# Two resident score buffers over five PSUM banks in the attention loop of a two-layer trunk

## The chip, the cores and the metric

The kernel runs on one core of a Trainium2 chip. The metric is device time in microseconds (us) from the first to the last instruction of one launch; lower is better. The core has a matrix engine (TensorE, PE in the rows; PEld is its weight load), a vector engine (VectorE, DVE), an activation engine (ScalarE, ACT), GpSimd (POOL) and a queue that issues DMAs (SyncE, SP). Matmul results land in PSUM, which has eight banks of 128 x 512 float32 each; VectorE and ScalarE read them there. TensorE's clock is granted at one of two levels, 1.2 or 2.4 GHz; the profile gives it as 0.5 or 1.0.

## The reference

Two layers over 1024 latent tokens and 256 context tokens of width 1024. Layer 0 is a gated linear recurrence beside a spatial gating unit. Layer 1 is a gated short convolution beside differential attention; the change lies in layer 1. Its attention, cut to what is needed here:

```python
def diff_attention(q, k, v, lam):          # 4 heads, two 64-wide maps m = 0, 1 per head
    s = jnp.einsum('bqhmd,bkhmd->bhmqk', q, k).astype(jnp.float32) * (DIFF_HEAD_DIM ** -0.5)
    p = jax.nn.softmax(s, axis=-1)          # over 1280 keys (256 context + 1024 latent)
    a = p[:, :, 0] - lam * p[:, :, 1]
    return jnp.einsum('bhqk,bkhe->bqhe', a.astype(v.dtype), v)
...
oo = rms_norm(oo, subln_g) * (1.0 - lam_init)
y_d = oo * jax.nn.silu(gate)                # then [y_c, y_d] @ w_out, residual, LayerNorm
```

Everything is float32. The kernel splits each float32 operand into a high and a low part (`split`: ScalarE makes the high part, VectorE or GpSimd subtracts for the low part) and multiplies with two or three matmuls.

## The kernel before

The program is one long list of instructions per engine. TensorE's order is the order of the code (`manual_schedule`); the other engines' orders are made by the scheduling layer, which also places the semaphore waits.

Layer 1 begins with projections for K and V (to about 602 us), then `run(proj_qg(0))`, the query and gate projection of head 0. Then comes the attention loop of 34 steps `i`, 32 of which work on one block of 128 queries of one head: `hd = i // 8`, block `i % 8`, `u = i % 2`. A step does, on TensorE:

- `scores(i, 0, st)`: six matmuls (128x256 or 128x512) that fill 1280 columns of a score tile `psc`. VectorE then takes the row maximum (`tensor_reduce`), and ScalarE the exponential of all 1280 columns with its row sum (`AF.Exp`, `accum_out`).
- for odd `i`, `av(i - 2)`: 30 matmuls of the probabilities with V into a bank `pav`; for even `i` sometimes `finish2` and `finish3`, the normalisation of a finished half head (`pms`, `prs`).
- `scores(i, 1, st)`: the second map. After it VectorE combines the two maps in `E0[i]`.
- `trans(i - 1, ..., j)` for j = 0, 1, 2: ten 128x128 transposes of the block before, four, four and two to a bank `atr`; each bank is read by ScalarE (`ah`) and VectorE (`al`).

Between these pieces `fill(us)` advances `fillers`, generators that project the other heads' queries and gates (`proj_qg`) and the convolution branch (`conv_branch`). A projection (`proj1_g`) is 24 matmuls of 128x512 into one bank, in eight groups of three. Fillers that are left when the loop ends run during the loads of the output weights (`out_weights`), before the output projection (`pout`).

Before the change the score tile `psc` is one buffer of three banks (`pa`), projections have two banks of their own (`pb`), and transposes, `pav`, `pms` and `prs` take turns in three banks: two of `ps1` (`psb`) and one of `pa` (`ps3`). K for one map is fetched into `kd` and split into `KS[m]` in one function, `load_k`; `kd` has one buffer, which `load_v` uses too.

Of the kernel before, what the change touches and what calls it, by code (L numbers as in the profile page):

```python
# [21 lines left out]
NTOK = CTX + LAT  # L22
KT = D // 128
# [19 lines left out]
def tile_hybrid_trunk(es: ExitStack, tc: tile.TileContext, A, out, scr=None):  # L43
# [110 lines left out]
    def run(gen):  # L154
        for _ in gen:
            pass
# [23 lines left out]
    def proj1_g(o, w, c0, n):  # L180
        hh, hl_ = hs(c0, n)
        for k in range(KT):
            hi, lo = w[k // 4]
            T.matmul(o, hi[:, k % 4], hh[:, k], start=k == 0, stop=False)  # L184
            T.matmul(o, hi[:, k % 4], hl_[:, k], start=False, stop=False)  # L185
            T.matmul(o, lo[:, k % 4], hh[:, k], start=False, stop=k == KT - 1)  # L186
            yield 0.65 * n / 512

    def proj1(o, w, c0, n):
# [559 lines left out]


    mask = [(i + 16) % 32 for i in range(32)]
    pa_cm, pb_cm = pool("pa", PSUM), pool("pb", PSUM)
    pbp, pa = pb_cm.__enter__(), pa_cm.__enter__()

    def pb(name):
        t = pbp.tile([128, 512], F32, name=name, tag="pb", bufs=2)
        return t

    kv_cm = pool("kv", side="right")
    kv = kv_cm.__enter__()  # L760
# [92 lines left out]
    def conv_branch(f):  # L853
# [25 lines left out]
        for c0 in (0, 512):  # L879
# [5 lines left out]
            V.tensor_tensor(u[:, c0:c0 + 512], u[:, c0:c0 + 512], s, op=ALU.mult)  # L885
            SY.dma_start(yc_d[f][:, c0:c0 + 512], u[:, c0:c0 + 512])

    ab_cm = pool("att")
    ap = ab_cm.__enter__()
    dl = ap.tile([128, 4, 64], F32, name="dl")  # L890
# [9 lines left out]
    gsub = lv[:, 6:7]  # L900
    V.tensor_scalar(gsub, P("subln"), 0.5 * (1.0 - LAM_INIT), None, op0=ALU.mult)

    def load_k(hd, m):
        kd = ap.tile([128, NTOK], F32, name="kd", tag="kd", bufs=1)
        for i in range(2):
            SY.dma_start(kd[64 * i:64 * i + 64], k_d[hd][64 * m:64 * m + 64])
        kt = ap.tile([128, NTOK], F32R, name=f"k{m}")
# [4 lines left out]
    def load_v(hd):  # L912
        vf = ap.tile([128, NT, 128], F32, name="vf", tag="kd", bufs=1)
        SY.dma_start(vf, v_d[:, :, 128 * hd:128 * hd + 128])
        vh = ap.tile([128, NT, 128], F32R, name="vh")
        vl = ap.tile([128, NT, 128], F32R, name="vl")
        split(vh, vl, vf, le=G)
        VS[0] = vh, vl

    def load_q(hd, pr):  # L920
# [17 lines left out]
            except StopIteration:  # L938
                fillers.pop(0)

    KS, VS, QS, AH, OF, SD = {}, {}, {}, {}, {}, {}

    turn = [0]

    def ps3(name):
        turn[0] += 1
        if turn[0] % 3:
            return psb(name)
        t = pa.tile([128, 512], F32, name=name, tag="ps3", bufs=1)
        return t  # L950

    def scores(i, m, st):
        hd, pr, u = i // 8, i % 8 // 2, i % 2
        qh, ql = QS[hd, pr]
        cu = slice(128 * u, 128 * u + 128)
        p = pa.tile([128, 1536], F32, name="psc", tag="psc", bufs=1)
        for c, n in CHUNKS:
            o = p[:, 256 + c:256 + c + n]
            T.matmul(o, qh[:, m, cu], KS[m][:, c:c + n], start=True, stop=False)  # L959
            T.matmul(o, ql[:, m, cu], KS[m][:, c:c + n], start=False, stop=True)  # L960
        V.tensor_reduce(st[:, m:m + 1], p[:, 256:1536], axis=AX.X, op=ALU.max, negate=True)  # L961
        e_ = ap.tile([128, NTOK], F32, name="e", tag="e", bufs=3)
        S.activation(e_, p[:, 256:1536], AF.Exp, bias=st[:, m:m + 1], scale=1.0, accum_out=st[:, 2 + m:3 + m])  # L963
# [60 lines left out]
    run(proj_qg(0))  # L1024
    fillers += [proj_qg(1), conv_branch(0), proj_qg(2), conv_branch(1), proj_qg(3), conv_branch(2), conv_branch(3)]
    load_k(0, 0)
    load_k(0, 1)
    E0, fin = {}, None
    for i in range(34):
        hd, pr, u = i // 8, i % 8 // 2, i % 2  # L1030
        if i < 32:
            if u == 0:
                QS[hd, pr] = load_q(hd, pr)
            st = ap.tile([128, 8], F32, name="st", tag="st", bufs=3)
            if i % 4 == 0:
                SD[i // 4] = ap.tile([128, 4], F32, name="sd", tag="sd", bufs=2)
            E0[i] = scores(i, 0, st)
            if i % 8 == 7 and hd < 3:
                load_k(hd + 1, 0)
        if i > 1 and u == 1:  # L1040
            fill(FL[1])
            av(i - 2)
            if i % 4 == 1:
                fin = ((i - 2) // 8, (i - 2) % 8 // 4, finish1((i - 2) // 8, (i - 2) % 8 // 4))
            if i % 8 == 1 and hd < 4:
                load_v(hd)
            fill(FL[2])
        elif fin is not None:
            fill(FL[0])
            fin2 = fin[0:2] + finish2(2 * fin[0] + fin[1], *fin[2])  # L1050
            fill(FL[3] - FL[0] - FL[8])
            finish3(*fin2)
            fill(FL[8])
            fin = None
        else:
            fill(FL[3])
        if i < 32:
            e1 = scores(i, 1, st)
            V.scalar_tensor_tensor(E0[i], e1, st[:, 6:7], E0[i], op0=ALU.mult, op1=ALU.add)
            if i % 8 == 7 and hd < 3:  # L1060
                load_k(hd + 1, 1)
        if i == 1:
            load_v(0)
# [27 lines left out]
    pb_cm.__exit__(None, None, None)  # L1091


    with pool("out1") as op, pool("po1", PSUM) as po:
# [148 lines left out]
```

## Time and profile before

| | |
|---|---|
| time, median of 3 runs (lowest to highest) | 1166.85 us (1166.33 to 1167.54) |
| the profiled execution: its time, its span | 1171.65 us, 1169.9 us |
| TensorE busy, share of the span | 1131.7 us, 97% |
| VectorE, ScalarE, GpSimd busy | 736.3, 440.3, 316.7 us |
| attention loop in the span | from 624 us to about 1046 us |
| mean granted clock of TensorE | 0.990 |

The rows of the trace give times in us from the start of the span of the profiled execution. Matmuls are pipelined: each row of one is longer than the distance to the next row's start, so for matmuls the distance between starts is the cost. A bracket such as [1.94 <-ACT e L963] says that the engine was idle for 1.94 us before that instruction, and what ended the wait.

### The profile page before, as it was taken

What the parts mean: (1) busy time and instruction counts of PE and PEld (TensorE: products, weight loads), DVE (VectorE), ACT (ScalarE), POOL (GpSimd) and SP (SyncE); (2) the same over time, 40 slices, a digit from 0 to 9 for tenths busy, and PEclk for the clock granted to TensorE, in tenths of its full rate; (3) what the DMA queues carried; (4) which work ended last, traced back from release to release, by engine and by line L of the source; (5) the groups of instructions that cost most, each with busy time, mean ns of one, the idle gap of its engine ahead of it and who ended that gap; (6) DMA issues with size and microseconds to landing.
All of it is one profiled execution on the core that took longest, in us unless ns stands there. A gap on an engine that the chain in (4) does not pass through costs nothing.

```text
span 1169.9 us, 14909 instructions
## 1 busy us (share of the span) xinstructions
PE 1131.7 (97%) x5842; PEld 925.4 (79%) x5842; DVE 736.3 (63%) x1007; ACT 440.3 (38%) x685; POOL 316.7 (27%) x200
## 2 busy tenths in 40 slices
PE   6999999999999999999998999999999899999997
PEld 3767777878888888888887888788788788888776
DVE  5677976943512665644015678786867777738897
ACT  3453654610221333341123555455534454413110
POOL 1111111630240222375014112222212121221971
PEclk9999999999999999999998999999989999999999
DMA  9654552230331534333126213222311410127622
GB/s 371 236 190 141 180 182 70 92 95 1 111 143 45 188 124 139 135 113 131 45 64 194 72 36 94 79 77 64 102 39 45 146 53 20 49 76 249 212 99 82
DMA packets 71095, 133.92 MB, mean 114 GB/s; under 512 B 5857, under 2 KB 34401, under 8 KB 70129
## 3 DMA queue, kind: packets, MB, share of 16 engines
q1 hardware_dynamic: 71024, 132.97, 33.9%
q8 instruction: 46, 0.75, 0.3%
q14 instruction: 25, 0.20, 0.0%
HBM read 105.67 MB, written 27.28 MB: 114 GB/s over the span
## 4 chain that ended last, share of the span: by engine, by line
PE 62%; DVE 7%; DMA 4%; POOL 3%; ACT 2%; issue 2%; SPq 0%; POOLq 0%; DVEq 0%; ACTq 0%
PE p L184 4%; PE p L185 4%; PE p L186 4%; PE pout L666 4%; PE pout L664 4%; PE pout L665 4%; PE pv L208 3%; PE pv L210 3%; PE pv L209 3%; PE psc L959 3%; PE psc L960 3%; PE atr L982 2%; POOL xres L1111 2%; PE pav L994 2%; PE pav L995 2%
## 5 line engine op out<-in xcount | busy, mean ns | idle before, releaser
L141 POOL TENSOR_TENSOR wlo<-wraw,whi 128x512 fp32r<-128x512 f32 x92 | 137.9, 1504 | 478.7 <-ACT whi L138 462.0
L666 PE MATMUL pout<-woh,ylo 128*128 128x512 f32 (+1 forms) x296 | 114.5, 387 | 3.8 <-DVE ylo L141 3.8
L961 DVE TENSOR_REDUCE st<-psc 128x1 f32<-128x1280 f32 x64 | 95.1, 1486 | 32.2 <-PE psc L960 32.1
L664 PE MATMUL pout<-woh,yhi 128*128 128x512 f32 (+1 forms) x296 | 114.8, 388 | 0.2
L665 PE MATMUL pout<-wol,yhi 128*128 128x512 f32 (+1 forms) x296 | 114.1, 385 | 0.0
L963 ACT ACTIVATE e<-psc,st 128x1280 f32<-128x1280 f32 x64 | 85.1, 1330 | 71.9 <-DVE st L961 71.2
L138 ACT ACTIVATE whi<-wraw 128x512 fp32r<-128x512 f32 x92 | 57.2, 627 | 135.9 <-PE p L185 31.6
L184 PE MATMUL p<-hhl,whi 128*128 128x512 f32 x256 | 105.7, 413 | 0.0
L186 PE MATMUL p<-hhl,wlo 128*128 128x512 f32 x256 | 101.5, 396 | 0.0
L185 PE MATMUL p<-hll,whi 128*128 128x512 f32 x256 | 101.2, 395 | 0.0
L959 PE MATMUL psc<-k,qh 128*128 128x512 f32 (+1 forms) x192 | 68.6, 372 | 12.7 <-ACT e L963 12.6
L960 PE MATMUL psc<-k,ql 128*128 128x512 f32 (+1 forms) x192 | 70.0, 365 | 0.0
L666 PEld LDWEIGHTS pout<-woh,ylo 128*128 128x128 f32 x296 | 55.6, 188 | 16.0 <-DVE ylo L141 4.6
L138 ACT ACTIVATE ah<-atr 128x512 fp32r<-128x512 f32 (+1 forms) x96 | 47.0, 525 | 52.2 <-PE atr L982 51.2
L664 PEld LDWEIGHTS pout<-woh,yhi 128*128 128x128 f32 x296 | 55.6, 188 | 12.3 <-issue 0.5
L665 PEld LDWEIGHTS pout<-wol,yhi 128*128 128x128 f32 x296 | 55.7, 188 | 11.4
L138 ACT ACTIVATE yhi<-yraw 128x512 fp32r<-128x512 f32 x36 | 22.5, 630 | 111.4 <-PE pout L665 62.2
L141 DVE TENSOR_TENSOR al<-atr,ah 128x512 fp32r<-128x512 f32 (+1 forms) x96 | 54.6, 593 | 6.1 <-ACT ah L138 5.9
L186 PEld LDWEIGHTS p<-hhl,wlo 128*128 128x128 f32 x256 | 48.7, 190 | 10.8
L185 PEld LDWEIGHTS p<-hll,whi 128*128 128x128 f32 x256 | 49.0, 191 | 8.6
L184 PEld LDWEIGHTS p<-hhl,whi 128*128 128x128 f32 x256 | 48.9, 191 | 8.4
L959 PEld LDWEIGHTS psc<-k,qh 128*128 128x128 f32 x192 | 36.6, 191 | 22.5 <-ACT e L963 17.9
(319 smaller groups left out, 2890.4 us busy)
## 6 DMA issues: line engine op xcount, KB each, us to landing
wraw<-in_w_in_dram SPq DMA_DIRECT2D x44, 512.0 KB, 4.5
wm<-in_w_mod_dram SPq DMA_DIRECT2D x64, 256.0 KB, 2.9
wraw<-in_w_out_dram SPq DMA_DIRECT2D x16, 512.0 KB, 3.6
wm<-in_w_mod_dram SPq DMA_DIRECT2D x7, 1024.0 KB
xt<-in_xcT_dram SPq DMA_DIRECT2D x8, 640.0 KB, 10.1
xres<-in_xc_dram SPq DMA_DIRECT2D x10, 512.0 KB, 3.7
kd<-k_d SPq DMA_DIRECT2D x16, 320.0 KB, 4.7
wvr<-in_w_v_dram SPq DMA_DIRECT2D x8, 512.0 KB, 3.6
```

What stands on the lines that cost most here:

```text
L138: S.activation(hi, src, AF.Copy)
L141: le.tensor_tensor(lo, src, f32(hi), op=ALU.subtract)
L184: T.matmul(o, hi[:, k % 4], hh[:, k], start=k == 0, stop=False)
L185: T.matmul(o, hi[:, k % 4], hl_[:, k], start=False, stop=False)
L186: T.matmul(o, lo[:, k % 4], hh[:, k], start=False, stop=k == KT - 1)
L664: T.matmul(o, hi[:, i], wh[:, c], start=first and i == 0, stop=False)
L665: T.matmul(o, hi[:, i], wl[:, c], start=False, stop=False)
L666: T.matmul(o, lo[:, i], wh[:, c], start=False, stop=not first and i == 3)
L959: T.matmul(o, qh[:, m, cu], KS[m][:, c:c + n], start=True, stop=False)
L960: T.matmul(o, ql[:, m, cu], KS[m][:, c:c + n], start=False, stop=True)
L961: V.tensor_reduce(st[:, m:m + 1], p[:, 256:1536], axis=AX.X, op=ALU.max, negate=True)
L963: S.activation(e_, p[:, 256:1536], AF.Exp, bias=st[:, m:m + 1], scale=1.0, accum_out=st[:, 2 + m:3 + m])
```

## The change

It has five parts.

1. `psc` becomes one resident tile `PSC` of 2560 columns, five banks: score 0 has columns 0 to 1279, score 1 columns 1280 to 2559. The third bank (columns 1024 to 1535) holds the last 256 columns of score 0 and the first 256 of score 1. The pieces of score 0 are written in the order 512, 512, 256, those of score 1 as before in the order 256, 512, 512.
2. The three other banks serve projections, transposes, `pav`, `pms` and `prs` together: `psb` gives out the one used longest ago, leaving out the bank of a projection that is under way. Before the loop (the K, V and first query projections) six banks rotate; then a pool is closed, and `PSC` is laid over its place.
3. The transposes move from behind score 1 to between the two scores, with fills of 1.4 and 0.4 around them; after score 1 only `fill(1.6 if u else 2.0)` is left.
4. K tiles are fetched two to three steps ahead (`fetch_k`, `kd` with two buffers), V right after a head's last step, and queries one step ahead. V's low part moves from GpSimd to VectorE, in two halves.
5. The square in `finish1` moves from VectorE to ScalarE.

```diff
@@ proj1_g, at the last k
+            if k == KT - 1:
+                bank["n"] += 1
+                last[bank["p"]] = bank["n"]
+                bank["p"] = None
@@
-    def psb(name="psb"):
-        t = ps1.tile([128, 512], F32, name=name, tag="psb", bufs=2)
+    def psb(name="psb", proj=False):
+        bank["n"] += 1
+        free = [b for b in last if b != bank["p"]]
+        b = min(free, key=last.get)
+        last[b] = bank["n"]
+        if proj:
+            bank["p"] = b
+        t = (ps1 if b < 2 else bank["pool"]).tile([128, 512], F32, name=name, tag=f"psb{b}", bufs=1)
         return t
@@
+    run(proj_qg(0))
+    pk_cm.__exit__(None, None, None)
+    for b in range(3, 6):
+        del last[b]
...
+    PSC = pa.tile([128, 2 * NTOK], F32, name="psc")
@@ load_v
-        split(vh, vl, vf, le=G)
+        for k in (0, 5):
+            split(vh[:, k:k + 5], vl[:, k:k + 5], vf[:, k:k + 5])
@@ scores
-        p = pa.tile([128, 1536], F32, name="psc", tag="psc", bufs=1)
-        for c, n in CHUNKS:
-            o = p[:, 256 + c:256 + c + n]
+        p = PSC[:, NTOK * m:NTOK * m + NTOK]
+        for c, n in (CHUNKS if m else ((0, 512), (512, 512), (1024, 256))):
+            o = p[:, c:c + n]
@@ finish1
-        V.tensor_tensor(sq, of, of, op=ALU.mult)
+        S.activation(sq, of, AF.Square)
@@ the loop
         if i > 1 and u == 1:
-            fill(FL[1])
+            fill(0.9)
             av(i - 2)
...
-            fill(FL[2])
+            fill(0.4)
...
         else:
-            fill(FL[3])
+            fill(3.6)
+        for js, us in (((0, 1), 1.4), ((2,), 0.4)):
+            for j in js:
+                if 1 <= i < 33:
+                    trans(i - 1, E0[i - 1], j)
+            fill(us)
         if i < 32:
             e1 = scores(i, 1, st)
...
-        fill(FL[4])
-        for js, us in (((0, 1), FL[5] + FL[6]), ((2,), FL[7])):
-            for j in js:
-                if 1 <= i < 33:
-                    trans(i - 1, E0[i - 1], j)
-            fill(us)
+        fill(1.6 if u else 2.0)
```

The first place is the end of a step on TensorE. Before, this is what stands behind score 1 of a step (`psc` from `k_4866`, the K tile of map 1): the rows begin at the last matmul of score 1 and end at the third piece of the transposes; three more projection matmuls follow, and then score 0 of the next step.

```order
L960 MATMUL psc<-k_4866,ql 128x512
L982 MATMUL atr<-ident,e 128x128 x8
L184 MATMUL p_5320<-hhl,whi 128x512
L185 MATMUL p_5320<-hll,whi 128x512
L186 MATMUL p_5320<-hhl,wlo 128x512
L184 MATMUL p_5320<-hhl,whi 128x512
L185 MATMUL p_5320<-hll,whi 128x512
L186 MATMUL p_5320<-hhl,wlo 128x512
L184 MATMUL p_5320<-hhl,whi 128x512
L185 MATMUL p_5320<-hll,whi 128x512
L186 MATMUL p_5320<-hhl,wlo 128x512
L982 MATMUL atr<-ident,e 128x128 x2
```

After the change the same place, with the semaphores that an instruction waits for; `k_4875` is the K tile of map 1, `k_4872` that of map 0.

```order
L984 MATMUL psc<-k_4875,ql 128x512
L184 MATMUL pg_5007<-hhl,whi 128x512
L185 MATMUL pg_5007<-hll,whi 128x512
L186 MATMUL pg_5007<-hhl,wlo 128x512 [waits Pool_49]
L184 MATMUL pg_5007<-hhl,whi 128x512
L185 MATMUL pg_5007<-hll,whi 128x512
L186 MATMUL pg_5007<-hhl,wlo 128x512
L184 MATMUL pg_5007<-hhl,whi 128x512
L185 MATMUL pg_5007<-hll,whi 128x512
L186 MATMUL pg_5007<-hhl,wlo 128x512
L983 MATMUL psc<-k_4872,qh 128x512 [waits Activation_49]
L984 MATMUL psc<-k_4872,ql 128x512
```

The transposes and a group of projection matmuls are gone from here, and the first matmul of score 0, which writes the first bank of `PSC`, waits for ScalarE. This wait stands in all 31 steps that follow another; the count it waits for is the one that the exponential of score 1 of the step before brings about. Nine projection matmuls stand between the two scores in 22 of these steps, six in eight and twelve in one. Over the whole loop, 897 projection matmuls stand between the first and the last score after the change, 861 before.

The second place is the transposes of an odd step after the change, behind the products with V (`pav`); `p_5158` is a projection.

```order
L1020 MATMUL pav<-ah,vl 128x256
L184 MATMUL p_5158<-hhl,whi 128x512
L185 MATMUL p_5158<-hll,whi 128x512
L186 MATMUL p_5158<-hhl,wlo 128x512
L1006 MATMUL atr<-ident,e 128x128 [waits DVE_49]
L1006 MATMUL atr<-ident,e 128x128 x3
L1006 MATMUL atr<-ident,e 128x128 [waits Activation_49]
L1006 MATMUL atr<-ident,e 128x128 x3
L184 MATMUL p_5158<-hhl,whi 128x512
L185 MATMUL p_5158<-hll,whi 128x512
L186 MATMUL p_5158<-hhl,wlo 128x512 [waits Pool_49]
```

Each bank of transposes now has a wait of its own for the engine that reads the bank's last content; before, the first eight transposes of a step stand behind a score, and in most steps without a wait.

The third place is SP's queue at the end of the loop: before, the last four loads of the output weights (`wraw` from `in_w_out_dram`) with what follows them; `xres` are the residual tiles, `yraw` the two branches' outputs, `rowln` the LayerNorm rows.

```order
L239 DMA wraw<-in_w_out_dram 128x1024 x2
L886 DMA yc_d<-uc 128x512
L1099 DMA rowln_g_8741<-in_ln_g_dram 128x1024
L239 DMA wraw<-in_w_out_dram 128x1024
L1099 DMA rowln_g_8743<-in_ln_g_dram 128x1024
L239 DMA wraw<-in_w_out_dram 128x1024
L1099 DMA rowln_b_8745<-in_ln_b_dram 128x1024
L1099 DMA rowln_b_8747<-in_ln_b_dram 128x1024
L886 DMA yc_d<-uc 128x512
L1110 DMA xres<-n_d 128x1024 x2
L250 DMA yraw<-yc_d 128x4x128
L1110 DMA xres<-n_d 128x1024
```

After the change, the same queue from the last LayerNorm row on.

```order
L1131 DMA rowln_b_8692<-in_ln_b_dram 128x1024
L1142 DMA xres<-n_d 128x1024 x2
L252 DMA wraw<-in_w_out_dram 128x1024
L1142 DMA xres<-n_d 128x1024
L899 DMA yc_d<-uc 128x512
L1142 DMA xres<-n_d 128x1024 x4
L899 DMA yc_d<-uc 128x512
L1142 DMA xres<-n_d 128x1024
L252 DMA wraw<-in_w_out_dram 128x1024
L263 DMA yraw<-yc_d 128x4x128 x2
L263 DMA yraw<-yd_d 128x4x128
L252 DMA wraw<-in_w_out_dram 128x1024
```

Three of the eight loads of the output weights now stand behind residual tiles, the last two behind all eight of them.

## Rows read from the trace of the kernel before

**Rows 1.** Page, part 1: busy us, share of the span, instructions of each engine.

```profile
PE 1131.7 (97%) x5842; PEld 925.4 (79%) x5842; DVE 736.3 (63%) x1007; ACT 440.3 (38%) x685; POOL 316.7 (27%) x200
```

**Rows 2.** Windows, attention loop and after: us, busy of each engine, clock, DMA share, GB/s.

```profile
624.00:1045.60 421.60, 408.31 (x2228) 346.83 (x2227) 297.92 (x413) 198.93 (x333) 88.65 (x58) 0.98 0.24 73
1045.60:1069.30 23.70, 23.70 (x108) 19.60 (x107) 22.21 (x24) 9.06 (x12) 2.58 (x2) 1.00 0.58 178
```

**Rows 3.** Waits of TensorE in the loop: us in total, times, longest.

```profile
PE psc L959 <- ACT e L963: 12.6, 9, 3.7
PE prs L1019 <- POOL rr L1011: 0.6, 1, 0.6
```

**Rows 4.** Groups by line, the two readers of a score: busy, mean ns | idle before.

```profile
L961 DVE TENSOR_REDUCE st<-psc 128x1 f32<-128x1280 f32 x64 | 95.1, 1486 | 32.2 <-PE psc L960 32.1
L963 ACT ACTIVATE e<-psc,st 128x1280 f32<-128x1280 f32 x64 | 85.1, 1330 | 71.9 <-DVE st L961 71.2
```

**Rows 5.** Timeline, one long wait for a score buffer: start us, us, engine, line.

```profile
741.38 0.39 PE L184 MATMUL p<-hhl,whi 128*128 128x512 f32 x1
...
741.61 0.40 PE L185 MATMUL p<-hll,whi 128*128 128x512 f32 x1
...
743.01 0.39 PE L960 MATMUL psc<-k,ql 128*128 128x512 f32 x1
743.04 3.27 DVE L1002 TENSOR_TENSOR sq<-of 128x512 f32<-128x512 f32 x1 [1.94 <-ACT of L997]
...
746.24 1.48 DVE L961 TENSOR_REDUCE st<-psc 128x1 f32<-128x1280 f32 x1
...
747.75 1.33 ACT L963 ACTIVATE e<-psc,st 128x1280 f32<-128x1280 f32 x1 [2.21 <-DVE st L961]
...
748.97 0.19 ACT L963 ACTIVATION_READ_ACCUMULATOR e<-psc,st 128x1 f32 x1
...
749.22 0.38 PE L959 MATMUL psc<-k,qh 128*128 128x256 f32 x1 [1.94 <-ACT e L963]
```

**Rows 6.** Timeline, a score whose readers are free, and two banks of transposes.

```profile
806.77 0.40 PE L960 MATMUL psc<-k,ql 128*128 128x512 f32 x1
...
807.01 1.04 PE L982 MATMUL atr<-ident,e 128*128 128x128 f32 x8
807.21 1.49 DVE L961 TENSOR_REDUCE st<-psc 128x1 f32<-128x1280 f32 x1 [0.39 <-PE psc L960]
...
807.64 1.09 ACT L138 ACTIVATE ah<-atr 128x512 fp32r<-128x512 f32 x2 [2.82 <-PE atr L982]
808.62 1.28 DVE L141 TENSOR_TENSOR al<-atr,ah 128x512 fp32r<-128x512 f32 x2
```

**Rows 7.** Windows, the stretches at half clock: the first of four, and their sum.

```profile
633.80:640.60 6.80, 6.02 (x15) 4.86 (x16) 4.66 (x12) 2.64 (x5) 3.87 (x3) 0.50 0.61 184
...
sum 20.40, PE 19.62 PEld 15.94 DVE 15.07 ACT 5.07 POOL 6.46; mean PE 4.90 PEld 3.99 DVE 3.77 ACT 1.27 POOL 1.61
```

**Rows 8.** Timeline, three of TensorE's nine waits for a score buffer.

```profile
634.58 0.58 PE L959 MATMUL psc<-k,qh 128*128 128x256 f32 x1 [3.71 <-ACT e L963]
...
712.76 0.39 PE L959 MATMUL psc<-k,qh 128*128 128x256 f32 x1 [1.08 <-ACT e L963]
...
847.94 0.39 PE L959 MATMUL psc<-k,qh 128*128 128x256 f32 x1 [1.97 <-ACT e L963]
```

**Rows 9.** Timeline, the readers of a gate projection's bank as the loop begins.

```profile
623.67 0.58 ACT L849 ACTIVATE sg<-pg 128x512 f32<-128x512 f32 x1
...
624.41 0.68 DVE L850 SCALAR_TENSOR_TENSOR sg<-sg,pg 128x512 f32<-128x512 f32 x1
```

**Rows 10.** Windows, the start of the output stage: columns as in rows 2.

```profile
1070.00:1090.00 20.00, 17.91 (x79) 14.44 (x78) 11.17 (x10) 4.61 (x6) 12.12 (x5) 1.00 0.98 347
```

**Rows 11.** Timeline, SP's queue in the output stage, and TensorE's first wait there.

```profile
1071.56 0.38 SPq L239 DMA_DIRECT2D wraw<-in_w_out_dram  x1
...
1073.76 1.16 SPq L1110 DMA_DIRECT2D xres<-n_d  x2
...
1089.08 0.50 PE L666 MATMUL pout<-woh,ylo 128*128 128x512 f32 x1 [2.09 <-DVE ylo L141]
```

More of the change, by code (lines that the diff above doesn't have):

```diff
@@ L212, in vtile @@
                 next(between, None)
-    def psb(name="psb"):
-        t = ps1.tile([128, 512], F32, name=name, tag="psb", bufs=2)
+    bank = {"n": 0, "p": None}
+    last = {0: 0, 1: 0}
+    def psb(name="psb", proj=False):
[6 more added lines that the diff above has]
+        t = (ps1 if b < 2 else bank["pool"]).tile([128, 512], F32, name=name, tag=f"psb{b}", bufs=1)
         return t
@@ L751, in tile_hybrid_trunk @@
     mask = [(i + 16) % 32 for i in range(32)]
-    pa_cm, pb_cm = pool("pa", PSUM), pool("pb", PSUM)
-    pbp, pa = pb_cm.__enter__(), pa_cm.__enter__()
+    pk_cm = pool("pk", PSUM)
+    bank["pool"] = pk_cm.__enter__()
+    last.update({b: 0 for b in range(2, 6)})
     def pb(name):
-        t = pbp.tile([128, 512], F32, name=name, tag="pb", bufs=2)
-        return t
+        return psb(name, True)
     kv_cm = pool("kv", side="right")
@@ L886, in conv_branch @@
             SY.dma_start(yc_d[f][:, c0:c0 + 512], u[:, c0:c0 + 512])
+    run(proj_qg(0))
+    pk_cm.__exit__(None, None, None)
+    for b in range(3, 6):
+        del last[b]
+    bank["p"] = None
+    pa_cm = pool("pa", PSUM)
+    pa = pa_cm.__enter__()
+    bank["pool"] = pa
+    PSC = pa.tile([128, 2 * NTOK], F32, name="psc")
     ab_cm = pool("att")
@@ L901, in tile_hybrid_trunk, with fetch_k, load_k @@
     V.tensor_scalar(gsub, P("subln"), 0.5 * (1.0 - LAM_INIT), None, op0=ALU.mult)
-    def load_k(hd, m):
-        kd = ap.tile([128, NTOK], F32, name="kd", tag="kd", bufs=1)
+    def fetch_k(hd, m):
+        kd = ap.tile([128, NTOK], F32, name="kd", tag="kd", bufs=2)
         for i in range(2):
             SY.dma_start(kd[64 * i:64 * i + 64], k_d[hd][64 * m:64 * m + 64])
+        KD[m] = kd
+    def load_k(m):
+        kd = KD.pop(m)
         kt = ap.tile([128, NTOK], F32R, name=f"k{m}")
@@ L910, in load_k, with fetch_v, load_v @@
         KS[m] = kt
-    def load_v(hd):
-        vf = ap.tile([128, NT, 128], F32, name="vf", tag="kd", bufs=1)
+    def fetch_v(hd):
+        vf = ap.tile([128, NT, 128], F32, name="vf", tag="kd", bufs=2)
         SY.dma_start(vf, v_d[:, :, 128 * hd:128 * hd + 128])
+        KD["v"] = vf
+    def load_v():
+        vf = KD.pop("v")
         vh = ap.tile([128, NT, 128], F32R, name="vh")
         vl = ap.tile([128, NT, 128], F32R, name="vl")
-        split(vh, vl, vf, le=G)
+        for k in (0, 5):
+            split(vh[:, k:k + 5], vl[:, k:k + 5], vf[:, k:k + 5])
         VS[0] = vh, vl
@@ L939, in fill @@
                 fillers.pop(0)
[L941 to L950, printed above, removed]
+    KS, VS, QS, AH, OF, SD, KD = {}, {}, {}, {}, {}, {}, {}
+    ps3 = psb
     def scores(i, m, st):
@@ L1022, in finish3 @@
         SY.dma_start(yd_d[hd][:, 512 * half:512 * half + 512], of)
-    run(proj_qg(0))
     fillers += [proj_qg(1), conv_branch(0), proj_qg(2), conv_branch(1), proj_qg(3), conv_branch(2), conv_branch(3)]
-    load_k(0, 0)
-    load_k(0, 1)
+    fetch_k(0, 0)
+    fetch_k(0, 1)
+    QS[0, 0] = load_q(0, 0)
+    load_k(0)
+    load_k(1)
+    fetch_v(0)
     E0, fin = {}, None
@@ L1031, in tile_hybrid_trunk @@
         if i < 32:
-            if u == 0:
-                QS[hd, pr] = load_q(hd, pr)
+            if u == 1 and i < 31:
+                QS[(i + 1) // 8, (i + 1) % 8 // 2] = load_q((i + 1) // 8, (i + 1) % 8 // 2)
+            if hd < 3 and i % 8 == 5:
+                fetch_k(hd + 1, 0)
+            if hd < 3 and i % 8 == 6:
+                fetch_k(hd + 1, 1)
             st = ap.tile([128, 8], F32, name="st", tag="st", bufs=3)
@@ L1038, in tile_hybrid_trunk @@
             if i % 8 == 7 and hd < 3:
-                load_k(hd + 1, 0)
+                load_k(0)
         if i > 1 and u == 1:
-            fill(FL[1])
+            fill(0.9)
             av(i - 2)
@@ L1045, in tile_hybrid_trunk @@
             if i % 8 == 1 and hd < 4:
-                load_v(hd)
-            fill(FL[2])
+                load_v()
+            fill(0.4)
         elif fin is not None:
-            fill(FL[0])
+            fill(0.7)
             fin2 = fin[0:2] + finish2(2 * fin[0] + fin[1], *fin[2])
-            fill(FL[3] - FL[0] - FL[8])
+            fill(2.9)
             finish3(*fin2)
-            fill(FL[8])
             fin = None
         else:
-            fill(FL[3])
+            fill(3.6)
[4 more added lines that the diff above has]
+            fill(us)
         if i < 32:
@@ L1060, in tile_hybrid_trunk @@
             if i % 8 == 7 and hd < 3:
-                load_k(hd + 1, 1)
+                load_k(1)
+                fetch_v(hd + 1)
         if i == 1:
-            load_v(0)
-        fill(FL[4])
-        for js, us in (((0, 1), FL[5] + FL[6]), ((2,), FL[7])):
-            for j in js:
-                if 1 <= i < 33:
-                    trans(i - 1, E0[i - 1], j)
-            fill(us)
+            load_v()
+        fill(1.6 if u else 2.0)
     fill(FL[0])
@@ L1090, in tile_hybrid_trunk @@
     pa_cm.__exit__(None, None, None)
-    pb_cm.__exit__(None, None, None)
+    del last[2]
+    bank["p"] = None
     with pool("out1") as op, pool("po1", PSUM) as po:
```

4 lines of the change are left out of this document (2 added, 2 removed).

## The prediction

> **What bounds the kernel now.** I read the page first: TensorE is busy for 97% of the span [rows 1], so time can come only from its idle time, from its clock, or go to new waits on it. The windows show where its idle time lies [rows 2]: in the attention loop it is busy for 408.31 of 421.60 us, idle for 13.3; the 23.7 us behind the loop, where the remaining projections run, have none. The waits name what it waits for [rows 3]: 12.6 us in nine waits for the exponential that reads the one score buffer, and 0.6 us once for GpSimd. The timeline shows how such a wait comes about [rows 5]: score 1 ends near 743.4, but VectorE is in the square of `finish1` (3.27 us) until 746.3, so the maximum runs at 746.24, the exponential at 747.75, and the next score 0 starts at 749.22, after 1.94 us of idleness. Last I looked at the clock: four stretches of the loop, 20.4 us together, have a granted clock of 0.5, the lower level [rows 7], and the first follows a wait of 3.71 us [rows 8]. The waits of 1.94, 1.97 and 2.45 us were followed by such a stretch too, that of 1.08 us wasn't.
>
> **What the change can give.** All waits of the loop are 12.6 + 0.6 = 13.2 us. The slow stretches hold 19.62 us of matmul work [rows 7], which at the full level would take half: 9.8 us. So the most that can be won in the loop is 23.0 us.
>
> **What it adds: a wait at each score 0.** Two buffers free score 0 from score 1 only if score 0 doesn't wait for the reader of score 1. As built it does: its first matmul waits for the exponential of the score 1 just before, in 31 steps. So what matters is how long that takes after score 1, and what TensorE does meanwhile. With free readers the chain is: the last matmul of score 1 starts at 806.77, the maximum at 807.21, 0.44 later [rows 6]; the maximum takes 1.49 [rows 4, 6]; the exponential follows 0.03 later (746.24 + 1.48 to 747.75), and from its start to the released matmul pass 749.22 - 747.75 = 1.47, which includes the read of the row sum [rows 5]. Sum: 0.44 + 1.49 + 0.03 + 1.47 = 3.43 us from the start of the last matmul. TensorE's own next slot is 0.23 after it (741.38 to 741.61) [rows 5], so 3.20 us must be covered.
>
> Before, ten transposes (eight take 0.8 us, from 807.01 to the next matmul) and 12 to 15 projection matmuls stood there: 1.0 + 12 x 0.23 = 3.8 us, enough unless a reader was late. Now nine, six or twelve projection matmuls stand there: 2.07, 1.38 or 2.76 us. The waits are 1.13 (22 steps), 1.82 (8) and 0.44 (once): 24.9 + 14.6 + 0.4 = 39.9 us. That is the floor, with both readers idle when a score ends. They aren't always: VectorE is busy for 297.92 of the loop's 421.6 us (0.71) and ScalarE for 198.93 (0.47) [rows 2]; with half of a typical 0.8 us instruction left on either, a score would wait 0.71 x 0.4 + 0.47 x 0.4 = 0.47 us more, 15 us over 31 steps. The square and the early fetches take load and late data out of this queue, V's low part puts some in; between 0 and 15 I take 8. **Term: +48 (40 to 55).**
>
> **Fewer banks.** Projections, transposes and `pav` now share three banks, one of which a projection holds. The second bank of transposes needs the bank that `pav` or an older piece has just left, the third piece that of the first. The trace has no such sharing; the nearest rows are the two banks at 807 [rows 6]: transposes start at 807.01, their first bank is free when half of VectorE's 1.28 us from 808.62 is done, 809.26, so 1.46 us after the eighth transpose's slot ends (807.80). The fill that now stands there is 1.4 us: 0.1 of wait if nothing is in the way. If ScalarE is inside an exponential (1.33 us [rows 4], up to once per step), up to 1.4 more. With ScalarE busy for 0.47 of the time and half an exponential left, 0.3; so 0.4 us for each of 32 blocks, 13 us, and 3 for projections that start in a bank just used. **Term: +16 (0 to 45).**
>
> **Start of the loop.** `PSC` lies over banks of the closed pool, so the first score waits until the last gate projection is read: 0.58 on ScalarE and 0.68 on VectorE [rows 9] with hops of the size above, 1.6 us on TensorE. **Term: +1.6 (0 to 4).**
>
> **Behind the loop.** 36 projection matmuls more (897 against 861) stand in the loop, 36 x 0.23 = 8.3 us. This moves work and costs nothing by itself, but the 23.7 us that cover the loads of the output weights [rows 2] shrink to 15.4. And SP's order is worse: before, the last weight load was issued at 1071.56, ahead of the first residual tile at 1073.76 [rows 11]; now two weight loads stand behind all eight residual tiles. Eight tiles of 512 KB at the 347 GB/s of that stretch [rows 10] take 12.1 us. The first three tiles' products with the upper half of the weights need none of these loads and hide part; before, the first wait there was 2.09 us [rows 11]. Between 0 and 16 I take 10. **Term: +10.**
>
> **Clock.** The four slow stretches cost 9.8 / 4 = 2.45 us each, and waits of 1.9 us or more brought them. Of 31 new waits between 1.1 and 2.5 I expect six to bring one: 15 us; none would be 0, all 31 would be 76. **Term: +15 (0 to 76).**
>
> The rest costs nothing: the square (0.7 us on ScalarE, eight times, in place of VectorE) and V's halves lie beside TensorE's work and are in the queueing term; if that cover is gone they cost their own 0.7 and 0.8 us each.
>
> **Sum:** -13.2 - 9.8 + 48 + 16 + 1.6 + 10 + 15 = +67.6 us, on the profiled span of 1169.9. The profiled execution took 1171.65, the median of the runs is 1166.85; I put the sum on the median: 1234.5, **1235 us**.
>
> **Rivals.**
>
> *Wait at the shared bank only.* The two scores share just the third bank. If the wait held back only the last two matmuls of score 0, which write it, four matmuls (4 x 0.23 = 0.92 us) would run first: waits of 0.21, 0.90 and none, 22 x 0.21 + 8 x 0.90 = 11.8, with queueing 20; at that length few bring the slow clock, 3. Sum -23 + 20 + 16 + 1.6 + 10 + 3 = +27.6: 1194 us. For it speaks the code: the first two banks of score 0 have no other reader. Against it: the built order has the wait on the first matmul. The Trainium skill (PSUM — Partial Sum Buffer, section Summary: rules for kernel authors) has software guard PSUM by bank and quadrant, not by address; it speaks against a layout in which two scores share a bank, and by it the guard would be needed at this bank alone, which gives the 1194. No row of before shows two tiles in one bank. Chance 0.08.
>
> *The chain is covered (other side).* If maximum and exponential ended within the fill, the score waits and their slow clock would fall away, and the banks, late for the same reason, would be at their lower bound: -23 + 1.6 + 10 = -11.4, 1155 us. It decides where the chain to cover is under about 2.4 us in place of 3.20 (0.37 us a step use up the 11.4). Speaks against it: the maximum and the exponential alone take 2.8 [rows 4]. Chance 0.04.
>
> *The clock stays low.* A wait in every step could bring a slow stretch in every step: 76 in place of 15, 1296 us. For it: each wait of 1.9 us or more did. Against it: most of the new waits are nearer 1.1, and the wait of 1.08 did not [rows 8]. The Trainium skill (TensorE: Matmul & The Clock Gate, section A second HAM failure mode: psum-queue depth-cycling) describes such a kernel, whose short idle times between groups of matmuls make the clock swing; by it the time is that of this rival, and the row of 1.08 us agrees only in part. Chance 0.10.
>
> **How the numbers follow.** Forecast 0.78. The range for eight in ten goes from 1208 (queueing and banks near their lower bounds, or part of the first rival) to 1266 (banks at 35 or half of the clock's bound). What a measurement of this kernel can tell from no change is about 0.2%. Faster: the second rival, 0.04; within 0.2%: 0.01, a mix between it and the first; slower: 0.95.
>
> **What the new profile would show.** Right: TensorE waits for the exponential some 31 times, 1.5 us on average, always before the first 512-wide matmul of score 0 and never before score 1; the reduction's idle time stays; waits of `atr` for VectorE and ScalarE appear; `pout` waits for ScalarE's `woh`. Wrong: if the waits for the exponential total less than 25 us, the chain or the cover was misread; if they are there but the time isn't, another term overstates; if the granted clock of the loop is under 0.9, the third rival holds.

## The result and the profile after

The changed kernel took 1250.93 us (median of 4 runs, 1249.59 to 1251.41) against 1167.07 us for the kernel before: ratio 1.0717 (95% interval 1.0699 to 1.0736), 83.9 us slower. The forecast was 1235 us in a range of 1208 to 1266.

The page of the kernel after, part 1 (answers to [rows 1]): busy us, share of the span, instructions.

```profile
PE 1146.2 (92%) x5842; PEld 924.4 (74%) x5842; DVE 737.3 (59%) x1007; ACT 449.0 (36%) x697; POOL 307.3 (25%) x196
```

TensorE does the same 5842 instructions, at 92% of the span in place of 97%. Windows of the kernel after: the attention loop (first score to last `prs`), what follows it, and what precedes it; columns as in [rows 2].

```profile
633.60:1107.60 474.00, 422.41 (x2266) 348.11 (x2267) 300.15 (x413) 205.81 (x340) 77.03 (x55) 0.99 0.19 60
1107.60:1248.80 141.20, 111.17 (x480) 89.97 (x478) 99.08 (x114) 18.96 (x26) 63.25 (x26) 0.89 0.39 136
0.00:633.60 633.60, 612.62 (x3099) 486.32 (x3099) 338.10 (x480) 224.27 (x331) 167.03 (x116) 1.00 0.40 136
```

The same three windows of the kernel before are these.

```profile
624.00:1046.00 422.00, 408.71 (x2231) 347.14 (x2230) 297.92 (x413) 199.00 (x333) 88.89 (x59) 0.98 0.24 73
1046.00:1169.90 123.90, 112.40 (x516) 92.83 (x514) 104.98 (x119) 20.14 (x27) 62.36 (x28) 0.99 0.47 159
```

The loop took 52.0 us more, of which 36 moved projection matmuls are 36 x 0.23 = 8.3: 43.7 net. What follows took 17.3 us more with those 8.3 us of work fewer: 25.6 net. The loop began 9.6 us later. Together these are 78.9 us, the difference of the two profiled spans; the medians differ by 5 us more, mostly because the profiled execution of before lay 4.6 us over this median. One of the six runs of the kernel with parts 4 and 5 alone (below) took 3186.94 us; its ratio leaves that run out, and no trace of it was kept.

TensorE's waits in the loop after the change (answers to [rows 3]).

```profile
PE psc L983 <- ACT e L987: 41.9, 31, 2.7
PE psc L983 <- DVE sg L863: 7.2, 1, 7.2
PE atr L1006 <- DVE of L1044: 3.9, 6, 1.6
PE atr L1006 <- ACT of L1021: 2.1, 3, 1.2
```

31 waits for the exponential, all before score 0, are most of it. One of them, in the timeline (answers to [rows 5, 6]):

```profile
854.18 0.39 PE L984 MATMUL psc<-k,ql 128*128 128x512 f32 x1
...
854.61 1.49 DVE L985 TENSOR_REDUCE st<-psc 128x1 f32<-128x1280 f32 x1 [0.33 <-PE psc L984]
...
856.19 1.33 ACT L987 ACTIVATE e<-psc,st 128x1280 f32<-128x1280 f32 x1
...
856.26 0.40 PE L186 MATMUL p<-hhl,wlo 128*128 128x512 f32 x1
...
857.66 0.50 PE L983 MATMUL psc<-k,qh 128*128 128x512 f32 x1 [1.00 <-ACT e L987]
858.00 0.40 PE L984 MATMUL psc<-k,ql 128*128 128x512 f32 x1
```

Score 1 starts its last matmul at 854.18; maximum and exponential follow with less than 0.1 us between them; score 0 is released at 857.66, 3.48 us later (3.43 in the prediction). Nine projection matmuls stand between. The reader should also see what the bracket leaves out: from the start of the matmul before the wait (856.26) to the second one behind it (858.00) pass 1.74 us; two slots of 0.23 are 0.46, so the wait costs 1.28 where 1.00 is counted. Of the 0.28, 0.17 lie ahead of it, since the row of 856.26 is 0.40 long and its slot 0.23, and 0.11 behind it, since the next matmul starts 0.34 later in place of 0.23. All 31 waits, read in the same way, cost 0.27 or 0.28 us more than is counted.

### The profile page after: what moved, and what is told of

Same layout as the page of the kernel before. It is cut to its first block, busy times and chain, and to the rows that moved or that the text cites. A ratio compares the mean times of both kernels' runs of the same rounds, so it can differ in the third digit from the quotient of the medians.

```text
span 1248.8 us, 14862 instructions
## 1 busy us (share of the span) xinstructions
PE 1146.2 (92%) x5842; PEld 924.4 (74%) x5842; DVE 737.3 (59%) x1007; ACT 449.0 (36%) x697; POOL 307.3 (25%) x196
## 5 line engine op out<-in xcount | busy, mean ns | idle before, releaser
L141 POOL TENSOR_TENSOR wlo<-wraw,whi 128x512 fp32r<-128x512 f32 x92 | 134.8, 1470 | 574.3 <-ACT whi L138 557.6
L677 PE MATMUL pout<-woh,yhi 128*128 128x512 f32 (+1 forms) x296 | 117.4, 397 | 16.6 <-ACT woh L138 16.5
L678 PE MATMUL pout<-wol,yhi 128*128 128x512 f32 (+1 forms) x296 | 116.7, 394 | 5.9 <-DVE wol L141 5.9
L983 PE MATMUL psc<-k,qh 128*128 128x512 f32 (+1 forms) x192 | 71.9, 382 | 49.1 <-ACT e L987 41.9
L138 ACT ACTIVATE ah<-atr 128x512 fp32r<-128x512 f32 (+1 forms) x96 | 48.9, 526 | 48.1 <-PE atr L1006 47.1
L679 PEld LDWEIGHTS pout<-woh,ylo 128*128 128x128 f32 x296 | 56.9, 192 | 11.6
L138 ACT ACTIVATE yhi<-yraw 128x512 fp32r<-128x512 f32 x36 | 22.4, 629 | 118.8 <-PE pout L678 78.6
L1006 PE MATMUL atr<-ident,e 128*128 128x128 f32 x320 | 49.2, 276 | 8.7 <-DVE of L1044 3.9
```

Source lines behind the costliest of these rows:

```text
L677: T.matmul(o, hi[:, i], wh[:, c], start=first and i == 0, stop=False)
L678: T.matmul(o, hi[:, i], wl[:, c], start=False, stop=False)
L679: T.matmul(o, lo[:, i], wh[:, c], start=False, stop=not first and i == 3)
```

## The experiments

All ratios are to the kernel before, on the same chip.

**Which part of the change costs.** First the transposes go back to where they stood, with all fills of the loop as before the change; the rest of the change stays.

```diff
-        for js, us in (((0, 1), 1.4), ((2,), 0.4)):   # ahead of score 1
...
+        for js, us in (((0, 1), FL[5] + FL[6]), ((2,), FL[7])):   # behind score 1, fills as before
```

> The changed kernel with the ten transposes put back behind score 1 and with the filler amounts of the kernel before; the two score buffers in one tile, the three shared banks, the fetches ahead and the square on ScalarE stay. Theory: the transposes and 12 or more projection matmuls stand between score 1 and score 0 again, 3.8 us against 3.20 to cover, so the waits for the exponential fall from 41.9 to under 10; the 36 moved projection matmuls stand behind the loop again, so the waits of the output stage fall from 22 us by about half; 1250.9 - 40 - 10 = about 1200, range 1185 to 1215. What is left over the kernel before (some 35 us) is then the price of three shared banks. Rival (two score buffers in one tile cost by themselves, wherever the transposes stand): waits for the exponential stay over 30 us and the time over 1230.

Measured: 1174.24 us, ratio 1.0049 (1.0032 to 1.0067), below the range given. The waits for the exponential are 0.3 us in all; the stretch behind the loop takes 124.1 us, as before (123.9). What the expectation had too high is what would be left: some 35 us for the banks, and half of the waits behind the loop. The kernel's loop:

```profile
630.80:1047.40 416.60, 404.75 (x2231) 341.32 (x2232) 288.77 (x408) 201.41 (x339) 76.13 (x54) 0.99 0.22 67
```

Second, the kernel before gets only parts 4 and 5 (fetches ahead, V's low part on VectorE, the square on ScalarE), and, in a kernel of its own, only the square.

```diff
+        for k in (0, 5):
+            split(vh[:, k:k + 5], vl[:, k:k + 5], vf[:, k:k + 5])
...
+            if u == 1 and i < 31:
+                QS[(i + 1) // 8, (i + 1) % 8 // 2] = load_q((i + 1) // 8, (i + 1) % 8 // 2)
+            if hd < 3 and i % 8 == 5:
+                fetch_k(hd + 1, 0)
...
-        V.tensor_tensor(sq, of, of, op=ALU.mult)
+        S.activation(sq, of, AF.Square)
```

> The kernel before (its buffers, banks, order and filler) with two parts of the change alone: K, V and q fetched a step or more ahead, V's low part in halves on VectorE; and the square on ScalarE. Theory: of the 12.6 us of waits for the exponential, 1.94 and 1.97 us come from the square on VectorE, 3.71 from V's load on ScalarE's queue at the start and 2.45 from K's; those 10.1 us go, with the clock's four slow stretches (up to 9.8 us): 1168 - 10 to 1168 - 20, so 1148 to 1158. Rival (the fetches put V's and K's transfers in front of the first q's, which makes the first score wait as in the changed kernel, 6 to 7 us): 1155 to 1165, with a wait at the first score. Rival (the waits only move to another late reader): 1165 to 1170.

Measured: 1157.96 us, ratio 0.9912 (0.9898 to 0.9926).

> The kernel before with the square on ScalarE alone. Theory: the waits of 1.94 and 1.97 us that stood behind the square go, and the slow stretch behind each (2.45 us): 1168 - 4 to 1168 - 9, so 1159 to 1164. Rival: no measurable change.

Measured: 1162.70 us, ratio 0.9946 (0.9933 to 0.9959). The waits in the loop of the kernel with both parts, against [rows 3]:

```profile
PE psc L968 <- ACT qh L138: 2.9, 1, 2.9
PE psc L968 <- ACT e L972: 1.9, 4, 1.1
PE prs L1028 <- POOL rr L1020: 0.8, 2, 0.6
```

The late readers are gone (12.6 to 1.9 us), and a new wait of 2.9 us for the first q stands there, as the rival with the transfers had it, at under half its size. So the 83.9 us divide, by the ratios: parts 4 and 5 gain 0.9%, some 10 us; the two buffers and the three shared banks at the old order cost 1.0049 - 0.9912, 16 us; moving the transposes with their filler costs 1.0717 - 1.0049, 78 us.

**Why score 0 waits for score 1.** Two kernels give the scores six banks, so that they share none, and leave two for everything else. In one they are two tiles of three banks, in the other a single tile.

```diff
-    PSC = pa.tile([128, 2 * NTOK], F32, name="psc")
+    PSC = [pa.tile([128, 1536], F32, name=f"psc{j}") for j in range(2)]      # two tiles
+    PSC = pa.tile([128, 3072], F32, name="psc")                              # or one tile
```

> The changed kernel with each score in a tile of its own of three banks (six banks in all), and so two banks given out by last use in place of three; order and filler stay. Theory (the wait goes with the tile): waits for the exponential under 10 us in place of 41.9; waits for banks grow from 9 to some 30 to 60 us, since the third piece of transposes and every projection now need a bank that has just been written; time 1205 to 1255. Rival (the score's own readers are late, whatever the buffers): waits for the exponential stay near 40 and the time rises over 1260.

> As the kernel with two tiles of three banks, but the six banks are one tile: the two scores share no bank, only the tile. Theory (what is tracked is the tile, not the bank): score 0 still waits for the exponential of the score 1 before it, some 31 times and 35 to 50 us in all, and the time is 35 to 60 us over that of the kernel with two tiles. Rival (what is tracked is the bank; the shared third bank is the cause): waits for the exponential vanish here too and both kernels take the same time within 5 us.

Measured: 1293.76 us, ratio 1.1069 (1.1014 to 1.1124), for two tiles, over the range; 1340.83 us, ratio 1.1481 (1.1428 to 1.1533), for one. The two longest entries of the waits, two tiles and then one:

```profile
PE atr L1006 <- DVE al L141: 46.5, 31, 3.0
PE pout L677 <- ACT woh L138: 16.5, 3, 7.2
```

```profile
PE atr L1006 <- DVE al L141: 46.3, 31, 3.0
PE psc L983 <- ACT e L987: 40.5, 31, 2.6
```

With two tiles no score waits for an exponential; with one it does 31 times, though no bank is shared. So the wait goes with the tile. The kernels differ by 47.1 us for 40.5 us of counted waits, 49 with 0.27 us more for each. The transposes' wait is the price of two banks, and nearly equal in both. The windows of the two loops, two tiles and then one:

```profile
627.10:1148.00 520.90, 444.81 (x2266) 360.41 (x2267) 302.69 (x416) 210.60 (x344) 78.92 (x56) 0.96 0.18 56
630.90:1198.20 567.30, 454.23 (x2268) 359.45 (x2268) 302.86 (x413) 208.59 (x340) 76.60 (x55) 0.95 0.16 50
```

Two banks cost more than the wait they save, and two tiles missed its range for two reasons. All waits of transposes in its loop are 66 us, where 30 to 60 were expected for banks. And the clock, which the expectation leaves out, was at the lower level for 46.8 us of that loop, 7.5 in the changed kernel's; half of the busy time in these stretches is 22.4 us against 3.7.

**What the wait costs when it is covered.** The same filler in each pair of steps, moved behind score 1:

```diff
-            fill(0.9)                       # odd steps: ahead of pav, behind it
-            fill(0.4)
-            fill(3.6)                       # even steps: behind score 0 (2.9 with finish2)
-        for js, us in (((0, 1), 1.4), ((2,), 0.4)):
-        fill(1.6 if u else 2.0)             # behind score 1
+            fill(0.0)
+            fill(0.0)
+            fill(2.4)                       # 1.7 with finish2
+        for js, us in (((0, 1), 1.4), ((2,), 0.4 if u == 0 else 0.1)):
+        fill(3.2)
```

> The changed kernel with the same filler in each pair of steps, but all of it that can move put between score 1 and the next score 0 (3.2 us in place of 1.6 and 2.0). Theory (score 0 waits for the exponential of the score 1 just before it, because both lie in one tile, and what is late is the chain of 3.43 us that only filler behind score 1 can cover): the 41.9 us of waits for the exponential fall below 10 and with them some 0.27 us a step of restart, 31 steps; the time falls by 35 to 50 us, to 1200 to 1216. Rival (the banks are what costs: three banks given out by last use): filler moved away from the transposes makes their waits longer, and the time falls by less than 20 us. Rival (loop is even, the loss lies before and behind it): no change within 10 us.

Measured: 1218.57 us, ratio 1.0427 (1.0377 to 1.0477): 32 us gained, just short of the range. The waits for the exponential fell from 41.9 to 4.1 us, but others grew:

```profile
632.70:1079.20 446.50, 423.39 (x2268) 351.55 (x2268) 301.09 (x413) 203.91 (x340) 86.53 (x55) 0.98 0.20 64
```

The loop's idle time is 446.5 - 423.39 = 23.1 us, down by 28.5 from 51.6: some 9 us came back, most of it as waits for banks and for GpSimd.

**What the second buffer is worth.** Both orders again with one score buffer of three banks, as in the kernel before, and five banks by last use.

```diff
-    for b in range(3, 6):
+    for b in range(5, 6):
         del last[b]
-        p = PSC[:, NTOK * m:NTOK * m + NTOK]
+        p = pa.tile([128, 1536], F32, name="psc", tag="psc", bufs=1)[:, 256:1536]
```

> The changed kernel with one score buffer of three banks, as before the change, and so five banks given out by last use in place of three; order and filler stay. Theory (two buffers in one tile work like one at score 0: it waits for the exponential of the score just before in either case): the waits of score 0 stay, 31 of them, 40 to 50 us; those of the transposes for banks (9 us, and some 5 us of restarts) go, and the first score's wait falls from 7 us to under 4: 1250.9 - 14 - 4, so 1228 to 1242. Rival (the second buffer does help): the waits for the exponential rise over 60 us, since score 1 waits too, and the time is over 1250.

Measured: 1243.09 us, ratio 1.0631 (1.0613 to 1.0648), 1 us over the range; its waits at score 0:

```profile
PE psc L982 <- ACT e L986: 47.2, 31, 3.2
PE psc L982 <- ACT qh L138: 2.9, 1, 2.9
```

No transpose waits for a bank now, 5.3 us more are waited at score 0, and the loop's granted clock fell to 0.97: 23.9 us at the lower level, 7.5 in the changed kernel. By the ratios the gain is 10 us, by the medians 8; some 4 to 6 of it lie ahead of the loop, where the first score's wait fell from 7.2 to 2.9.

> The kernel with the filler behind score 1 (1218.6 us), with one score buffer and five banks. Theory (what is left there in the loop is 19 us of waits for banks, and the second score buffer buys nothing): the bank waits fall to under 4 us, waits for the exponential stay under 13, the first score's wait falls too; 1218.6 - 15 to 1218.6 - 28, so 1190 to 1204. Rival (the transposes' waits come from late readers and not from the number of banks): 1213 to 1222.

Measured: 1196.69 us, ratio 1.0240 (1.0220 to 1.0260), 22 us under the same order with two buffers. So in both orders the second buffer in the same tile loses time: its two more banks are missed elsewhere.

**The output stage.** 0.52 us less filler in each even step leaves it for behind the loop.

```diff
-            fill(2.9)
+            fill(2.38)
-            fill(3.6)
+            fill(3.08)
```

> The changed kernel with 0.52 us less filler in each even step, so that some 36 projection matmuls (8.3 us) stand behind the loop again as before the change; the rest of the change stays. Theory (the output stage waits because the filler that covers the weight loads was used up in the loop, and weight loads stand behind residual tiles): the stage's waits for weights fall from 22 us to under 8 and its slow clock (about 10 us) goes; the matmuls only change place; the time falls by 15 to 28 us, to 1223 to 1236. Rival (the waits of the output stage come from something else in the change): no change within 5 us.

Measured: 1234.65 us, ratio 1.0562 (1.0537 to 1.0587), 16 us gained. The stretch behind the loop:

```profile
1102.30:1227.30 125.00, 114.51 (x525) 94.50 (x523) 106.31 (x119) 20.75 (x28) 63.16 (x28) 0.99 0.46 158
```

It holds 45 matmuls more than the changed kernel's (45 x 0.23 = 10.4 us) and is 16.2 us shorter, at a granted clock of 0.99 in place of 0.89: 26.6 us gained here, with waits of 3.0 us in place of 22.4. On SP's queue all weight loads stand ahead of the residual tiles again. The loop gives part of it back: without these 10.4 us of work it is only 3.0 us shorter (471.0 us), and 19.4 us of it ran at the lower clock, 7.5 in the changed kernel.

**The start of the loop.** Filler ahead of the first score, in the kernel with the transposes back.

```diff
+    fill(5.2)
     E0, fin = {}, None
...
-            fill(FL[3])
+            fill(FL[3] - 0.33)              # likewise with finish2
```

> The kernel with the transposes back (1174 us) with 5.2 us of filler put ahead of the first score and taken back in 0.33 us pieces from the filler of the later steps. Theory (the 6.4 us wait of the first score is late work that TensorE could cover): the wait falls to about 1 us and the time by 4 to 7 us, to 1167 to 1170. Rival (the wait moves on to the next thing that is late, or the thinner filler brings new waits): 1172 to 1176.

Measured: 1170.80 us, ratio 1.0022 (1.0008 to 1.0035), 3.4 us gained, just short of the range: the first score's wait is gone, but 3.3 us of waits for the exponential stand in the loop where 0.3 were; the waits for banks (some 11 us) stay.

**All three moves of filler, and the best version.** The filler behind score 1, ahead of the first score and for the end together; then parts 4 and 5 on the kernel before, with the filler ahead of the first score.

> The changed kernel with three moves of filler together: behind score 1, 5.2 us ahead of the first score, and some 36 projection matmuls kept for behind the loop. Theory (the terms add: -32 measured for the first, -16 for the last, -4 for the one ahead): 1250.9 - 52 = 1199, range 1192 to 1206; what is left over the kernel before is the price of three banks with the transposes between the scores. Rival (thinner filler uncovers the chain or the banks again): over 1206, with waits for the exponential over 10 us.

Measured: 1195.59 us, ratio 1.0236 (1.0191 to 1.0281), as the sum of the terms has it. What waits in its loop:

```profile
PE prs L1043 <- POOL rr L1035: 11.6, 7, 3.0
PE atr L1006 <- ACT of L1021: 8.3, 8, 1.9
PE psc L983 <- ACT e L987: 3.5, 9, 0.6
```

The exponential's chain is covered; the thin filler around `finish2` uncovers the power that GpSimd takes there (`rr`, 11.6 us), and the waits for the three banks stay.

> The kernel before with the fetches ahead and the square on ScalarE (1158 us), with 5.2 us of filler ahead of the first score, taken back in 0.33 us pieces from the later steps. Theory: the first score's wait for its q (2.9 us) goes: 1154 to 1157. Rival (the thinner filler behind score 0 uncovers other waits of the same size): 1157 to 1161.

Measured: 1155.02 us, ratio 0.9881 (0.9864 to 0.9898): 1.2% faster than the kernel before, the best of all. Its loop is busy for 391.80 of 397.30 us:

```profile
631.20:1028.50 397.30, 391.80 (x2201) 334.85 (x2200) 286.55 (x404) 199.66 (x338) 75.46 (x52) 1.00 0.22 70
```

## Why the prediction came out as it did

The main mechanism was right: score 0 waits for the exponential of the score 1 before it, in 31 steps, for a chain that the filler no longer covers. The chain was 3.48 us (3.43 predicted), the usual waits, as counted, 0.95 to 1.05 and 1.64 to 1.73 us (1.13 and 1.82).

- **Wait at score 0, +48.** Right, and in its parts. The prediction reckons from slot to slot (a slot is the distance between two starts, 0.23 us here); the count starts 0.17 us later, where the longer row of the matmul before ends. From slot to slot the 31 waits are 46.9 us in place of the 41.9 counted: the floor of 39.9 and 7.0 for late readers, where 8 was predicted. But these come in few waits and not in each: seven hold 5.9 us. At 802.53 and 871.70, the two longest, VectorE was in other work and started the maximum 1.94 and 2.17 us after the last matmul of score 1, in place of 0.43. Left out were the 0.11 us behind each wait, 3.3 in all. The term is 50.
- **Banks, +16.** The trace counts 9.2 us in 16 waits of transposes and projections, some 13 with what the count leaves out. With five banks these waits were gone: that loop was 3.1 us shorter, though 5.3 us more were waited at score 0 and half of the busy time at the lower clock grew from 3.7 to 11.2 us. Added up this is 16 us, an estimate. At the old order, buffers and banks cost 16 with the start in it. Right in size.
- **Start of the loop, +1.6 (0 to 4).** Mis-sized: 7.2. (The loop began 9.6 us later, but 2.3 of that arose before the query projection, at 604.46 in place of 602.19; the kernel with the transposes back, of the same code there, has 602.41.) The prediction took the term as the two readers of the last gate bank. The rows of ScalarE, VectorE and SP there show what it left out:

```profile
616.76 0.58 SPq L940 DMA_DIRECT2D vf<-v_d  x1
...
620.97 1.10 SPq L928 DMA_DIRECT2D kd<-k_d  x2
622.12 0.58 SPq L145 DMA_DIRECT2D wraw<-in_w_in_dram  x1
622.74 2.55 SPq L954 DMA_DIRECT2D qd<-q_d  x4
```

```profile
629.65 0.63 ACT L138 ACTIVATE qh<-qd 128x512 fp32r<-128x512 f32 x1 [6.23 <-DMA qd<-q_d]
...
632.23 0.58 ACT L862 ACTIVATE sg<-pg 128x512 f32<-128x512 f32 x1
632.84 0.69 DVE L863 SCALAR_TENSOR_TENSOR sg<-sg,pg 128x512 f32<-128x512 f32 x1 [0.83 <-ACT sg L862]
633.58 0.29 PEld L983 LDWEIGHTS psc<-k,qh 128*128 128x128 f32 x1 [7.61 <-DVE sg L863]
```

The fetches ahead put V's and two K transfers in SP's queue in front of the first q, whose split on ScalarE waits until 629.65; the gate's tanh stands behind that split, and `PSC` waits for the tanh's reader. In four kernels with the fetches whose first score does not wait for the gate's reader, it waits 2.9 to 3.0 us for the split of q; in the five in which it does, 6.4 to 7.2. That the transfers ahead are what delays q was not tried by itself. So what the prediction left out is that the tanh itself comes late: it counted the early fetches only as load taken off the readers, and at this one place they cost.
- **Behind the loop, +10 (0 to 16).** Mis-sized: 25.6. The cause was right (cover used up, loads behind residual tiles), and with the filler kept the stretch was 26.6 us better. The waits there are 22.4 us:

```profile
PE pout L677 <- ACT woh L138: 16.5, 3, 9.5
PE pout L678 <- DVE wol L141: 5.9, 4, 2.1
```

In the kernel before they are 3.8 us:

```profile
PE pout L666 <- DVE ylo L141: 3.8, 2, 2.1
```

The step that failed is that the first three tiles' products with the upper half need none of the late loads. The prediction counted the two loads behind all eight residual tiles; the first of the three behind any of them is a weight of the upper half. SP's queue, VectorE's scaling of it and TensorE:

```profile
1123.62 0.82 SPq L1131 DMA_DIRECT2D rowln_g<-in_ln_g_dram  x2
1124.49 0.90 SPq L1131 DMA_DIRECT2D rowln_b<-in_ln_b_dram  x2
1125.44 0.94 SPq L1142 DMA_DIRECT2D xres<-n_d  x2
1126.57 0.42 SPq L252 DMA_DIRECT2D wraw<-in_w_out_dram  x1
```

```profile
1137.82 3.28 DVE L256 TENSOR_TENSOR wraw<-wraw,gl 128x1024 f32<-128x1024 f32 x1 [6.37 <-DMA wraw<-in_w_out_dram]
...
1142.24 0.79 PE L677 MATMUL pout<-woh,yhi 128*128 128x512 f32 x1 [9.51 <-ACT woh L138]
```

The load is issued at 1126.57 behind four LayerNorm rows and two residual tiles, is used from 1137.82 on, and holds the first tile's product until 1142.24. And the clock fell here, which cost 6.3 us (next term): 22.4 - 3.8 + 6.3 = 24.9 of the 25.6.
- **Clock, -9.8 and +15.** The half-clock stretches of the kernel after (answers to [rows 7]): two in the loop, two in the output stage.

```profile
630.50:637.30 6.80, 3.72 (x10) 3.05 (x11) 3.07 (x4) 2.15 (x4) 2.50 (x2) 0.52 0.88 251
872.80:876.20 3.40, 3.40 (x13) 2.86 (x12) 2.28 (x2) 1.08 (x1) 0.00 (x0) 0.55 0.00 0
1128.80:1149.20 20.40, 7.55 (x15) 4.86 (x16) 8.69 (x6) 2.32 (x3) 19.78 (x8) 0.51 1.05 394
1166.40:1173.20 6.80, 5.09 (x12) 3.80 (x12) 5.61 (x4) 0.28 (x1) 6.80 (x3) 0.52 0.11 33
```

Half of the busy time in them was lost: (3.72 + 3.40) / 2 = 3.6 us in the loop, (7.55 + 5.09) / 2 = 6.3 behind it. The loop thus lost 6.2 us less to the clock than before. Of the expected six slow stretches from 31 waits one came, behind the longest wait, that of 871.70; the other in the loop goes with the wait of 7.2 us at its start. So the +15 was mis-sized, 3.6 in the loop, and the sum of both clock terms, +5.2, is in truth about 0, with its loss in the output stage. That each wait of 1.9 us or more brings a slow stretch holds neither here (802.53) nor in the kernel before, where none followed the 2.09 us of [rows 11].

```profile
802.53 0.50 PE L983 MATMUL psc<-k,qh 128*128 128x512 f32 x1 [2.54 <-ACT e L987]
...
871.70 0.50 PE L983 MATMUL psc<-k,qh 128*128 128x512 f32 x1 [2.74 <-ACT e L987]
```

- **Waits removed, -13.2.** They went: 1.9 us are left of 12.6 in the kernel with parts 4 and 5 alone. With the clock the prediction had -23; that kernel gained 14 us between profiled spans, 9 between medians. The prediction put a sum made on a profiled execution of 1171.65 us onto the median; 4.8 us of the miss are that.

In the loop the terms add up: 50 + 13 for the score and bank waits, less 13.2 + 2.7 for the ten waits that went and 6.2 for the clock, are 41 of its 43.7 us. That the total came within 16 us of 1235 is in part luck: the stage behind the loop was 16 us dearer than predicted and the clock in the loop 11 us cheaper, and the two nearly cancel.

Of the rivals, the wait at the shared bank only is out: with no bank shared, one tile still makes score 0 wait. The Trainium skill (PSUM — Partial Sum Buffer, section Summary: rules for kernel authors) asks for a guard by bank; here the scheduling layer guards the whole tile, and the 40.5 us measured with one tile of six banks decide. The rival with a covered chain did not come as the kernel was built; the chain was covered only after filler had been moved. The clock that stays low did not come either: 0.99 in the loop, and 0.95 in the worst kernel tried.

## What to carry to other kernels

Count as one buffer what is one tile to the layer that places the semaphores: two halves of a tile are not two buffers, and two real ones must be paid for with banks that others need. Work that looks movable may be the cover of a chain; before moving it, add up the chain from the last write to the release and what TensorE still has in between. Filler spent in one place is missing in another: here 8.3 us of it cost 25.6 us at the end, and keeping it there won 16 us of the time back.

## What the runs showed of the hardware

A wait on TensorE costs more than its counted idle time: 0.27 or 0.28 us more at each of the 31 score waits of the changed kernel, 0.17 of it because the row of the matmul before is longer than its slot, and 0.11 because the first matmul behind the wait takes 0.34 us to the next start in place of 0.23.

Waits of 1.0 to 1.7 us once in about 14 us left the granted clock of the loop at 0.99, and one of 2.54 us at 802.53 brought no slow stretch, while those of 2.74 us at 871.70 and of 2.08 and 2.69 us at 1126.59 and 1130.02 stand at the start of one. More waits brought more: in the loop of one tile of six banks, with 95 of them in 567 us, the clock was at the lower level for 53.7 us (0.95 on average).
